# Attention scores as three fp32r terms on stacked rows, head outputs feature-major in column halves, and new state-space and gate stages in a hybrid decoder block

## The chip, the cores and the metric

The kernel runs on one core of one Trainium2 chip. A core has a matrix engine (TensorE, here PE; its weight loads are listed apart as PEld), a vector engine (VectorE, DVE), an activation engine (ScalarE, ACT), GpSimd (POOL) and SyncE (SP), which here only issues transfers. Each engine works its instructions off in the order in which the program holds them. The metric is device microseconds of one execution; lower is better.

## The reference

One decoder layer on 512 tokens of width 2048, everything in float32:

```
h = rms_norm(x);  q, k, v, u = split(h @ W_in)
attention, 16 heads of 64:  q, k rms-normed per head
    logits = q.k * scale - slope_h * distance, causal;  softmax;  @ v
state space, 64 groups of 16 channels, 64 complex states per group:
    scan over tokens;  y = Re(C s) + D u;  g = gelu(y)
    s_out = g * sigmoid(g @ W_glu + b)
x = x + concat(rms_norm(attn), rms_norm(s_out)) @ W_out
x = x + relu(rms_norm(x) @ W1)^2 @ W2          (W1: 2048 x 8192)
```

With 512 tokens in two blocks of 256 the block selection of the reference keeps every past block, so attention is plain causal attention with a linear distance penalty.

## The kernel before, in words

All matrix products with a weight matrix are made of three fp32r matmuls. A float32 operand is split into a rounded high part and the remainder, both in fp32r, and low times high, high times low and high times high are summed (`panel`, L114). `load_w` brings 256 rows of 512 weight columns with one transfer on SP's queue, `split_w` (L105) makes the two parts (copy on ACT, subtraction on DVE), and each step of 128 rows issues 12 matmuls of 512 columns into four PSUM banks.

The order of work on each engine is written by a planner when the program is built: it replays the program in a timing simulation of its own and gives each free engine the ready instruction that stands first in the program; what lies in `with hi()` goes first. So the program order is attention first and the next panel second, and on PE the panel's matmuls fill in wherever attention's next step is not ready.

The stages, in program order:

1. **State space** (`build`, `run`, `post`, L441 to L562), 16 rounds of four groups, among the two u panels (`uproj`) and the panels of the first half of q, k, v. `build` makes per-round matrices: four float32 matmuls into `kps` (L482), one after the other in 16 partitions of the bank, one copy to `kev`, a transfer to memory and back as `m3`. `run` brings in the tokens, makes `vps` (L513, two groups in the lower and upper 64 partitions), runs the scan on DVE and makes `yps` (L542 and L543, 64 output partitions, one group after another), which one copy brings to `ysb`. `post` transposes and applies GELU with three ACT and three DVE operations (L556 to L562); it stores twice the GELU, and later steps multiply by 0.5.
2. **Head norms** (`head_norm_T`, L623): for each of four row blocks of q and k, sum of squares per head, a reciprocal square root by integer guess and three Newton steps (`rsqrt_mean`, L168, 14 small DVE instructions), scaling, transposes.
3. **Attention** (L671), two halves of four head pairs. For each pair, each of four row blocks `i` and each head `e`: scores in float32 on the 64 rows of that head (L685), `sps`; one DVE operation that adds the penalty and takes the row minimum (L690; q is negated, so scores have the other sign); exponential on ACT with row sums (L692); transposes of the tile (`pps`, L696); a copy (L698); outputs in float32 with the transposed probabilities as weights and 64 columns of v moving (L701). At the end of a pair the outputs are divided by the row sums and stored token-major in `o_sb`. POOL makes the two heads' penalty tiles (L679). `sps`, `pps` and `ops` have one PSUM bank each, the score tile `sm` three buffers. The first half stands ahead of the panels of the second half of q, k, v; the second half stands ahead of the gate's panels (L733) and the panels of W_out for the state-space part (L772).
4. **Gate** (L732): one over one plus exp(-x) by ACT, an addition and a DVE reciprocal, times the GELU, split into high and low.
5. **W_out**: four panels on the state-space rows ("z"), then the attention outputs are transposed (L795), scaled and split, and four panels follow on the attention rows ("a").
6. **Feed-forward**, L830 to the end.

Thirteen buffers of 1 MB (`page`) hold the large activations; a tile that asks for one waits until one is free. `x1`, four pages loaded from memory on SP's queue, is needed where the z panels are added to the residual.

Of the kernel before, what the change touches and what calls it, by code (L numbers as in the profile page):

```python
# [45 lines left out]
def hybrid_block_kernel(ctx, tc, x, norm1_gain, w_in, q_norm_gain, k_norm_gain,  # L46
# [121 lines left out]
    def rsqrt_mean(dst, ssq, n, shape):  # L168

        v = small.tile(shape, F32, name="rv", tag="rv")  # L170
        w = small.tile(shape, F32, name="rw", tag="rw")
# [55 lines left out]
    nbglu = const.tile([P, 8], F32, name="nbglu")  # L227
# [9 lines left out]
    with ExitStack() as sx:  # L237
# [203 lines left out]
        def build(b):  # L441
# [37 lines left out]
            S.copy(bst[LO, :, 1], bbi[HI, js])  # L479
            kps = aux("kps", "bx")  # L480
            for q in range(4):
                PE.matmul(kps[:GH, q * P:(q + 1) * P], bst[:, q // 2, q % 2, :],  # L482
                          s2[:, q // 2, q % 2, 0:8, :].rearrange("p s h -> p (s h)"), start=True, stop=True)
            kev = st("kev", (GH, 8, 4, GH))
            S.copy(kev, kps[:GH].rearrange("p (g s h) -> p s g h", g=4, s=8))
# [17 lines left out]
        def run(b, ysb):  # L503
# [34 lines left out]
            V.tensor_add(xs[LO, :, 1, 1:], a1[HI, 1], a2[HI, 1])  # L538
            yps = aux("yp", "rx")
            for q in range(4):  # L540
                o = yps[:NCH, q * P:(q + 1) * P]
                PE.matmul(o, u[:, q, :], m3[:, :, q, :], start=True, stop=False)  # L542
                PE.matmul(o, xs[:, q // 2, q % 2, 0:NCH],  # L543
                          s2[:, q // 2, q % 2, 1:9, :], start=False, stop=True)
            hf = b % 2
            S.copy(ysb[:, :, 4 * hf:4 * hf + 4, :],
                   yps[:NCH].rearrange("c (g t h) -> c t g h", g=4, t=TC))

        def post(k, ysb):
# [5 lines left out]
            y = st("sy", (P, 512), bufs=2)  # L555
            S.copy(y, ps)  # L556
            a = st("sy", (P, 512), bufs=2)
            S.activation(a, y, AF.Square)
            V.tensor_scalar(a, a, 0.044715, 1.0, op0=ALU.mult, op1=ALU.add)
            V.tensor_mul(a, a, y)  # L560
            S.activation(a, a, AF.Tanh, scale=math.sqrt(2.0 / math.pi))
            V.scalar_tensor_tensor(s0t(k), a, 1.0, y, op0=ALU.add, op1=ALU.mult)  # L562
# [45 lines left out]
        V.tensor_scalar(nbglu, vt[:, 32:40], -1.0, None, op0=ALU.mult)  # L608
# [14 lines left out]
    def head_norm_T(ps4, dst, gain):  # L623
        for m in range(4):
# [5 lines left out]
            ss = small.tile([P, 8], F32, name="ss", tag="ss")  # L630
            V.tensor_reduce(ss, sq.rearrange("p (h d) -> p h d", d=DH), axis=AX.X, op=ALU.add)
            rs = small.tile([P, 8], F32, name="rs", tag="rs")
            rsqrt_mean(rs, ss, DH, [P, 8])
            qv = q.rearrange("p (h d) -> p h d", d=DH)
            V.tensor_mul(qv, qv, bc(rs, 2, DH))
            ps = ax("qt")
            for pr in range(4):
                PE.transpose(ps[:, pr * P:(pr + 1) * P], q[:, pr * P:(pr + 1) * P], ident)
# [30 lines left out]
    o_sb = [ap_.tile([P, 2, 1024], F32, name=f"o{i}") for i in range(2)]  # L669

    def attention(hf, qT, kT, vv):  # L671
        for pr in range(4):
            ops = aux("ops", "ops")
            rsum = small.tile([P, 4, 2], F32, name="rsum", tag="rsum")
            pen = []
            for e in range(2):
                slope = 2.0 ** (-8.0 * (hf * 8 + 2 * pr + e + 1) / H)
                pen.append(ap_.tile([P, 512], F32, name="pen", tag="pen", bufs=2))
                G.tensor_scalar(pen[e], dist, slope, 0.0, op0=ALU.mult, op1=ALU.add)  # L679
            for i in range(4):  # L680
                n = (i + 1) * P
                for e in range(2):
# [376 lines left out]
```

## Time and profile before

| | |
|---|---|
| median of 3 runs | 2156.73 us (2155.82 to 2157.74) |
| profiled execution | 2154.98 us |
| its span, first to last instruction | 2153.1 us |
| PE busy | 2113.7 us (98%) |
| DVE busy | 1517.7 us (70%) |
| ACT busy | 818.6 us (38%) |
| POOL busy | 199.6 us (9%) |
| granted PE clock, mean | 0.996 |

Busy time counts instructions from start to end; on PE they overlap, so the share says little on how close PE is to its rate, and the distance from one start to the next says more. A group's row gives line, engine, operation, tiles, shapes, count, then busy time and mean nanoseconds of one, then the idle time of the engine just before and what ended it. A float32 matmul is listed as two instructions, an fp32r matmul as one.

### The profile page before, as it was taken

The numbers are of one execution on the slowest core, as the hardware profiler recorded it, in microseconds if no ns is written. First come the engines' busy times: TensorE is split into PE (matmuls) and PEld (weight loads), VectorE is DVE, ScalarE is ACT, GpSimd is POOL, SyncE is SP. The second block draws the span as 40 slices with busy tenths as digits, with TensorE's granted clock in tenths as the row PEclk, the third lists the DMA queues.
The fourth block names the chain that finished last, engine by engine and source line by source line (L and its number), as shares of the span: only waits on it lengthen the run. The fifth ranks groups of instructions, "written<-read, shape, count | busy, mean of one in ns | idle before, by whom it ended". The sixth has DMA issues, their size and how long they took to land.

```text
span 2153.1 us, 26096 instructions
## 1 busy us (share of the span) xinstructions
PE 2113.7 (98%) x9905; PEld 1711.1 (79%) x9905; DVE 1517.7 (70%) x2514; ACT 818.6 (38%) x1295; POOL 199.6 (9%) x291
## 2 busy tenths in 40 slices
PE   8889999999999999999999999999999999999998
PEld 6667777777777888888888888888888888888887
DVE  6889993435475444677777777777777777877767
ACT  5233443444454343333333333333333333333332
POOL 1486650000020000000000000000000000000000
PEclk9999999999999999999999999999999999999999
DMA  6332222212132441233332333333333333333332
GB/s 196 108 91 86 80 89 88 69 59 69 59 118 78 135 140 40 82 104 96 110 104 92 117 98 98 118 98 98 115 101 98 108 108 98 99 114 97 95 114 98
DMA packets 149613, 213.51 MB, mean 99 GB/s; under 512 B 15672, under 2 KB 82320, under 8 KB 148976
## 3 DMA queue, kind: packets, MB, share of 16 engines
q1 hardware_dynamic: 136240, 201.36, 29.7%
q10 hardware_dynamic: 12416, 8.92, 1.4%
q0 software_dynamic: 832, 1.57, 0.3%
q8 instruction: 78, 1.28, 0.3%
q14 instruction: 47, 0.39, 0.1%
HBM read 204.54 MB, written 7.27 MB: 98 GB/s over the span
## 4 chain that ended last, share of the span: by engine, by line
PE 87%; DVE 8%; issue 1%; DMA 1%; POOL 1%; ACT 1%; SPq 0%; ACTq 0%; DVEq 0%; POOLq 0%
PE f L865 11%; PE f L866 11%; PE f L867 11%; PE g L961 9%; PE g L963 9%; PE g L959 9%; PE mm L133 6%; PE mm L132 6%; PE mm L134 6%; PE sps L685 2%; PE ops L701 2%; PE mm L136 1%; DVE wl L111 1%; PE mm L137 1%; PE mm L138 1%
## 5 line engine op out<-in xcount | busy, mean ns | idle before, releaser
L846 ACT CAST th<-w 128x1024 fp32r<-128x1024 f32 x349 | 361.7, 1054 | 644.9 <-PE g L963 467.3
L847 DVE TENSOR_TENSOR tl<-w,th 128x1024 fp32r<-128x1024 f32 x349 | 425.9, 1221 | 63.0 <-ACT th L846 63.0
L969 DVE TENSOR_TENSOR x<-x,g 128x512 f32<-128x512 f32 x434 | 294.0, 684 | 241.3 <-PE g L963 240.7
L865 PE MATMUL f<-h2h,tl 128*128 128x512 f32 x1024 | 398.5, 389 | 0.0
L866 PE MATMUL f<-h2l,th 128*128 128x512 f32 x1024 | 398.5, 389 | 0.0
L867 PE MATMUL f<-h2h,th 128*128 128x512 f32 x1024 | 398.4, 389 | 0.0
L961 PE MATMUL g<-tl,lf 128*128 128x512 f32 x868 | 337.9, 389 | 0.5 <-DVE tl L847 0.5
L963 PE MATMUL g<-th,lf 128*128 128x512 f32 x868 | 337.7, 389 | 0.0
L959 PE MATMUL g<-th,lf 128*128 128x512 f32 x868 | 320.0, 389 | 0.0
L111 DVE TENSOR_TENSOR wl<-raw,wh 128x512 fp32r<-128x512 f32 x208 | 150.9, 730 | 170.5 <-ACT wh L110 170.0
L867 PEld LDWEIGHTS f<-h2h,th 128*128 128x128 f32 x1024 | 192.2, 188 | 39.9
L865 PEld LDWEIGHTS f<-h2h,tl 128*128 128x128 f32 x1024 | 192.2, 188 | 39.8
L866 PEld LDWEIGHTS f<-h2l,th 128*128 128x128 f32 x1024 | 192.2, 188 | 39.8
L110 ACT CAST wh<-raw 128x512 fp32r<-128x512 f32 x208 | 128.3, 620 | 201.9 <-PE mm L134 127.5
L961 PEld LDWEIGHTS g<-tl,lf 128*128 128x128 f32 x868 | 162.9, 188 | 35.0 <-DVE tl L847 1.3
L959 PEld LDWEIGHTS g<-th,lf 128*128 128x128 f32 x868 | 163.0, 188 | 33.8
L963 PEld LDWEIGHTS g<-th,lf 128*128 128x128 f32 x868 | 162.9, 188 | 33.8
L132 PE MATMUL mm<-wh,xl 128*128 128x512 f32 x384 | 153.9, 402 | 0.5 <-DVE sy L582 0.5
L133 PE MATMUL mm<-wl,xh 128*128 128x512 f32 x384 | 154.2, 402 | 0.0
L134 PE MATMUL mm<-wh,xh 128*128 128x512 f32 x384 | 153.7, 401 | 0.0
L874 ACT ACTIVATE r<-r 128x512 f32<-128x512 f32 x64 | 40.0, 628 | 146.5 <-DVE r L873 146.5
L133 PEld LDWEIGHTS mm<-wl,xh 128*128 128x128 f32 x384 | 72.5, 189 | 21.5 <-issue 7.5
(344 smaller groups left out, 2723.4 us busy)
## 6 DMA issues: line engine op xcount, KB each, us to landing
w<-in_w_ff_dram SPq DMA_DIRECT2D x256, 512.0 KB, 3.8
raw<-in_w_in_dram SPq DMA_DIRECT2D x64, 512.0 KB, 3.7
raw<-in_w_out_dram SPq DMA_DIRECT2D x32, 512.0 KB, 3.6
x<-in_x_dram SPq DMA_DIRECT2D x7, 1024.0 KB, 11.7
m<-kp ACTq DMA_DIRECT2D x16, 256.0 KB, 3.3
raw<-in_w_glu_dram SPq DMA_DIRECT2D x8, 512.0 KB, 3.6
out_dram<-x SPq DMA_DIRECT2D x16, 256.0 KB, 2.2
ud<-sy ACTq DMA_DIRECT2D x8, 256.0 KB, 2.1
```

The source lines that it names most:

```text
L132: PE.matmul(ps[m], xl[:, ms], wh, start=st, stop=False)
L133: PE.matmul(ps[m], xh[:, ms], wl, start=False, stop=False)
L134: PE.matmul(ps[m], xh[:, ms], wh, start=False, stop=sp)
L846: S.copy(th, src)
L847: V.tensor_sub(tl, src, th.bitcast(F32))
L865: PE.matmul(ps[m], wl[:, k % 4, ms], xh_, start=k == 0, stop=False)
L866: PE.matmul(ps[m], wh[:, k % 4, ms], xl_, start=False, stop=False)
L867: PE.matmul(ps[m], wh[:, k % 4, ms], xh_, start=False, stop=k == 15)
L959: PE.matmul(ps[t], al_, th[:, q, :], start=first and q == 0, stop=False, skip_group_check=True)
L961: PE.matmul(ps[t], ah_, tl[:, q, :], start=False, stop=False, skip_group_check=True)
L963: PE.matmul(ps[t], ah_, th[:, q, :], start=False, stop=q == 1, skip_group_check=True)
L969: V.tensor_add(xs, xs, ps[t])
```

## The change

- **Scores.** `head_parts` makes, for each head, a tile `qhl` of 128 rows: the high part of q (divided by the head's slope) in its own 64 rows, the low part in the other 64; `khh`, the high part of k in both; `klo`, the low part of k in its own rows and zeros in the others. Two fp32r matmuls over 128 rows then give high.high + low.high + high.low. The DVE operation multiplies the penalty by the slope itself, so POOL's penalty tiles go.
- **Normalisation ahead.** The reciprocal of the row sum is taken per tile on DVE, and POOL scales the probabilities before they are transposed.
- **Outputs feature-major.** v is now the weight (64 columns) and the transposed probabilities move (128 columns); the two heads of a pair write the lower and upper 64 partitions of one bank, issued in turn. A copy on ACT stores the pair in `oraw`; the transposes ahead of the a panels go. The squares for the row norm are summed over features and brought into a row sum by small matmuls with ones (`row_rstd`), as for the state-space part.
- **State space.** `kps` writes four groups of 32 partitions, with four copies instead of one; `yps` writes two halves of 64 partitions, with two copies. GELU is one activation (tanh form) from PSUM into its place, without the factor two.
- **Head norms.** One `rsqrt_mean` for the four row blocks of a panel instead of four.
- **Gate.** The four banks of a panel are copied by DVE into a page, then four sigmoids follow on ACT; squares for the norm go from ACT to DVE. The split of the GELU's output goes wholly to DVE.

```diff
@@ build
-                PE.matmul(kps[:GH, q * P:(q + 1) * P], bst[:, q // 2, q % 2, :],
+                PE.matmul(kps[32 * q:32 * q + GH, 0:P], bst[:, q // 2, q % 2, :],
...
-            S.copy(kev, kps[:GH].rearrange("p (g s h) -> p s g h", g=4, s=8))
+            for q in range(4):
+                S.copy(kev[:, :, q, :], kps[32 * q:32 * q + GH, 0:P].rearrange("p (s h) -> p s h", s=8))
@@ run
-            for q in range(4):
-                o = yps[:NCH, q * P:(q + 1) * P]
-                PE.matmul(o, u[:, q, :], m3[:, :, q, :], start=True, stop=False)
-                PE.matmul(o, xs[:, q // 2, q % 2, 0:NCH],
-                          s2[:, q // 2, q % 2, 1:9, :], start=False, stop=True)
+            for j in range(2):
+                o = [yps[64 * e:64 * e + 64, j * P:(j + 1) * P] for e in range(2)]
+                for e in range(2):
+                    PE.matmul(o[e], u[:, 2 * j + e, :], m3[:, :, 2 * j + e, :], start=True, stop=False)
+                for e in range(2):
+                    PE.matmul(o[e], xs[:, j, e, 0:NCH], s2[:, j, e, 1:9, :], start=False, stop=True)
...
@@ post
-            y = st("sy", (P, 512), bufs=2)
-            S.copy(y, ps)
-            a = st("sy", (P, 512), bufs=2)
-            S.activation(a, y, AF.Square)
-            V.tensor_scalar(a, a, 0.044715, 1.0, op0=ALU.mult, op1=ALU.add)
-            V.tensor_mul(a, a, y)
-            S.activation(a, a, AF.Tanh, scale=math.sqrt(2.0 / math.pi))
-            V.scalar_tensor_tensor(s0t(k), a, 1.0, y, op0=ALU.add, op1=ALU.mult)
+            S.activation(s0t(k), ps, AF.Gelu_apprx_tanh)
@@ attention
+    def head_parts(qT, kT, pr, e, inv):
+        own, oth = slice(e * DH, (e + 1) * DH), slice((1 - e) * DH, (2 - e) * DH)
+        qhl = ap_.tile([P, 512], F32R, name="qhl", tag="qhl", bufs=2)
+        khh = ap_.tile([P, 512], F32R, name="khh", tag="khh", bufs=2)
+        q, k = qT[own, pr, :], kT[own, pr, :]
+        S.activation(qhl[own], q, AF.Copy, scale=inv)
+        V.scalar_tensor_tensor(qhl[oth], q, inv, qhl[own].bitcast(F32), op0=ALU.mult, op1=ALU.subtract)
+        V.tensor_copy(khh[own], k)
+        V.tensor_copy(khh[oth], k)
+        V.tensor_sub(klo[e][own], k, khh[own].bitcast(F32))
+        return qhl, khh
...
-                    PE.matmul(sps[:, :n], qT[rows, pr, i * P:(i + 1) * P], kT[rows, pr, 0:n],
-                              start=True, stop=True)
+                    PE.matmul(sps[:, :n], qhl[:, i * P:(i + 1) * P], khh[:, 0:n], start=True, stop=False)
+                    PE.matmul(sps[:, :n], qhl[:, i * P:(i + 1) * P], klo[e][:, 0:n], start=False, stop=True)
...
+                    rinv = small.tile([P, 1], F32, name="rinv", tag="rinv")
+                    V.reciprocal(rinv, rsum)
+                    G.tensor_scalar(sm[:, :n], sm[:, :n], rinv, 0.0, op0=ALU.mult, op1=ALU.add)
...
-                    for b in range(i + 1):
-                        PE.matmul(ops[:, o:o + DH], pt[:, b * P:(b + 1) * P],
+                for b in range(i + 1):
+                    for e in range(2):
+                        PE.matmul(oT[e * DH:(e + 1) * DH, i * P:(i + 1) * P],
                                   vv[:, b, pr * P + e * DH:pr * P + (e + 1) * DH],
-                                  start=b == 0, stop=b == i)
+                                  pts[e][:, b * P:(b + 1) * P], start=b == 0, stop=b == i)
+            with hi():
+                S.copy(oraw[:, pr, :], oT)
@@ gate
+        gate = page("gate")
+        with hi():
+            for m in range(4):
+                V.tensor_copy(gate[:, m, :], ps[m])
+            for m in range(4):
+                S.activation(gate[:, m, :], gate[:, m, :], AF.Sigmoid, bias=vt[:, 32 + 4 * n + m:33 + 4 * n + m])
...
-                e = t2("ge")
-                S.activation(e, ps[m], AF.Exp, bias=nbglu[:, k:k + 1], scale=-1.0)
-                V.tensor_scalar(e, e, 1.0, None, op0=ALU.add)
-                V.reciprocal(e, e)
@@ ahead of the a panels
-    for k in range(8):
-        ps = aux("ot", "tx")
-        for i in range(4):
-            PE.transpose(ps[:, i * P:(i + 1) * P], o_sb[i // 2][:, i % 2, k * P:(k + 1) * P], ident)
-        scaled_split(ah[k // 4][:, k % 4, :], al[k // 4][:, k % 4, :], ps, ga[:, k:k + 1])
+    for k in range(8):
+        o = oraw[k // 4][:, k % 4, :]
+        scaled_split(ah[k // 4][:, k % 4, :], al[k // 4][:, k % 4, :], o, ga[:, k:k + 1])
+        if k == 0:
+            S.activation(rbc, o, AF.Square)
+        else:
+            oq = t2("oq")
+            S.activation(oq, o, AF.Square)
+            G.tensor_add(rbc, rbc, oq)
+    rstda = row_rstd(rbc, "a")
```

More of the change, by code (lines that the diff above doesn't have):

```diff
@@ L168, in rsqrt_mean @@
     def rsqrt_mean(dst, ssq, n, shape):
-        v = small.tile(shape, F32, name="rv", tag="rv")
-        w = small.tile(shape, F32, name="rw", tag="rw")
+        v = ssq
+        w = small.tile([P, 32], F32, name="rw", tag="rw", bufs=1)
+        w = w[:, :math.prod(shape[1:])]
+        if len(shape) == 3:
+            w = w.rearrange("p (a b) -> p a b", b=shape[2])
         V.tensor_scalar(v, ssq, 1.0 / n, EPS, op0=ALU.mult, op1=ALU.add)
@@ L226, in hybrid_block_kernel @@
     kgain = vt[:, 41:42]
-    nbglu = const.tile([P, 8], F32, name="nbglu")
     qgain = const.tile([P, 1], F32, name="qgain")
@@ L623, in head_norm_T @@
     def head_norm_T(ps4, dst, gain):
+        qs = []
+        ss = small.tile([P, 4, 8], F32, name="ss", tag="ss", bufs=1)
         for m in range(4):
@@ L668, in hybrid_block_kernel @@
                     fill=1e33, base=384, channel_multiplier=1)
-    o_sb = [ap_.tile([P, 2, 1024], F32, name=f"o{i}") for i in range(2)]
-    def attention(hf, qT, kT, vv):
-        for pr in range(4):
[L673 to L679, printed above, removed]
+    klo = [ap_.tile([P, 512], F32R, name=f"klo{e}") for e in range(2)]
@@ new lines, in hybrid_block_kernel @@
+    for e in range(2):
+        V.memset(klo[e].bitcast(F32)[(1 - e) * DH:(2 - e) * DH], 0.0)
+    def head_parts(qT, kT, pr, e, inv):
[9 more added lines that the diff above has]
+        return qhl, khh
@@ L680, in attention @@
+    def attention(hf, qT, kT, vv, oraw):
+        for pr in range(4):
+            oT = aux("ops", "ops")
+            slope = [2.0 ** (-8.0 * (hf * 8 + 2 * pr + e + 1) / H) for e in range(2)]
+            parts = [head_parts(qT, kT, pr, e, 1.0 / slope[e]) for e in range(2)]
             for i in range(4):
                 n = (i + 1) * P
+                pts = []
                 for e in range(2):
-                    rows = slice(e * DH, (e + 1) * DH)
+                    qhl, khh = parts[e]
@@ L691, in attention @@
                                            op0=ALU.add, op1=ALU.min, accum_out=mn)
-                    S.activation(sm[:, :n], sm[:, :n], AF.Exp, bias=mn, scale=-1.0,
-                                 accum_out=rsum[:, i, e:e + 1])
+                    rsum = small.tile([P, 1], F32, name="rsum", tag="rsum")
+                    S.activation(sm[:, :n], sm[:, :n], AF.Exp, bias=mn, scale=-1.0, accum_out=rsum)
+                    rinv = small.tile([P, 1], F32, name="rinv", tag="rinv")
+                    V.reciprocal(rinv, rsum)
@@ L720, in hybrid_block_kernel @@
         with hi():
-            S.activation(h_, s0t(k), AF.Copy, scale=0.5)
-            V.scalar_tensor_tensor(l_, s0t(k), 0.5, h_.bitcast(F32), op0=ALU.mult, op1=ALU.subtract)
-    attention(1, *qkv1)
+            V.tensor_copy(h_, s0t(k))
+            V.tensor_sub(l_, s0t(k), h_.bitcast(F32))
+    oraw.append(page("oraw1"))
+    attention(1, *qkv1, oraw[1])
     def sact(k):
@@ L733, in hybrid_block_kernel @@
         ps = panel(w_glu, 0, 8, n * 512, sact, False)
+        gate = page("gate")
+        with hi():
+            for m in range(4):
+                V.tensor_copy(gate[:, m, :], ps[m])
+            for m in range(4):
+                S.activation(gate[:, m, :], gate[:, m, :], AF.Sigmoid, bias=vt[:, 32 + 4 * n + m:33 + 4 * n + m])
         for m in range(4):
```

82 lines of the change are left out of this document (35 added, 47 removed).

## The prediction

> **What bounds the kernel now.** I read the page first (busy shares, the forty slices, the chain), then a table of stretches, then the order of time on the matrix engine (PE).
>
> ```profile
> PE 2113.7 (98%) x9905; PEld 1711.1 (79%) x9905; DVE 1517.7 (70%) x2514; ACT 818.6 (38%) x1295; POOL 199.6 (9%) x291
> PE   8889999999999999999999999999999999999998
> DVE  6889993435475444677777777777777777877767
> PE 87%; DVE 8%; issue 1%; DMA 1%; POOL 1%; ACT 1%; SPq 0%; ACTq 0%; DVEq 0%; POOLq 0%
> ```
>
> PE is the chain for 87% of the span. The other 13% lies almost all in the first six slices, where DVE has 8s and 9s. The stretches below (columns: length, then busy time of PE, PEld, DVE, ACT, POOL, each with its count) are: the state-space stage with the u and first q, k, v projections; the attention stage; the remainder of the z projection; the feed-forward network.
>
> ```profile
> 85.00:323.00 238.00, 222.69 (x1359) 171.35 (x1358) 214.49 (x547) 95.97 (x211) 155.85 (x236) 0.98 0.30 88
> 358.00:688.00 330.00, 327.93 (x1579) 247.99 (x1579) 164.29 (x415) 148.65 (x334) 20.91 (x21) 1.00 0.24 75
> 688.00:741.00 53.00, 53.00 (x250) 44.17 (x250) 25.76 (x52) 18.91 (x38) 0.00 (x0) 1.00 0.28 90
> 813.00:2153.10 1340.10, 1333.75 (x5899) 1103.37 (x5897) 1000.38 (x1190) 472.35 (x547) 0.00 (x0) 1.00 0.32 100
> ```
>
> In 85 to 323 us PE (223 of 238) and DVE (214 of 238) are both nearly full: relieving one alone gives little there. In 358 to 741 PE has no idle time to speak of, and DVE and ACT are half idle: a microsecond of PE work less is a microsecond less, as long as other matmuls cover attention's waits. The last 1340 us hold nothing that the diff touches.
>
> How much cover is there? The two rows below are the projection matmuls alone, in the attention stage and in the stretch after it.
>
> ```profile
> 358.00:688.00 330.00, 234.94 (x934) 169.40 (x933) 2.72 (x4) 14.58 (x22) 1.00 0.24 75
> 688.00:741.00 53.00, 50.52 (x219) 40.89 (x219) 7.12 (x11) 0.00 (x0) 1.00 0.28 90
> ```
>
> For 64 score tiles (16 heads, 4 row blocks) 934 were used, 14.6 per tile; 219 were left when attention ended. So there are 1153/64 = 18 per tile.
>
> **Prices on PE.** A busy PE overlaps its own tails, so I price by start to start.
>
> ```profile
> 396.38 0.39 PE L133 MATMUL mm<-wl,xh 128*128 128x512 f32 x1
> 396.60 0.39 PE L134 MATMUL mm<-wh,xh 128*128 128x512 f32 x1
> 396.92 1.12 PE L685 MATMUL sps<-kT,qT 64*128 64x512 f32 x2
> 397.98 0.50 PE L132 MATMUL mm<-wh,xl 128*128 128x512 f32 x1
> ...
> 407.53 1.00 PE L701 MATMUL ops<-vv,pt 128*128 128x64 f32 x8
> 408.37 0.61 PE L696 MATMUL pps<-ident,sm 128*128 128x128 f32 x4
> 408.90 0.48 PE L685 MATMUL sps<-kT,qT 64*128 64x128 f32 x2
> 409.32 0.50 PE L133 MATMUL mm<-wl,xh 128*128 128x512 f32 x1
> ...
> 292.96 0.38 PE L542 MATMUL yp<-m,u 128*64 128x128 f32 x2
> 294.27 0.38 PE L542 MATMUL yp<-m,u 128*64 128x128 f32 x2
> 294.58 0.50 PE L133 MATMUL mm<-wl,xh 128*128 128x512 f32 x1
> ...
> 303.39 0.73 PE L513 MATMUL vp<-u,m1t 128*64 128x64 f32 x16
> 304.05 0.50 PE L132 MATMUL mm<-wh,xl 128*128 128x512 f32 x1
> ```
>
> - An fp32r matmul of 512 columns steps 0.22 to 0.23 us: I use 0.227.
> - An fp32 pass of 128 columns (a float32 matmul is two instructions) steps 0.109: twelve between 292.96 and 294.27.
> - The change from 64 output columns to 128 costs: 294.27 plus two passes is 294.49, the next begins at 294.58, so 0.09 at each side of such a group. The same 0.09 lies between 396.60 + 0.227 and 396.92.
> - A score tile takes from 396.83 to 397.98 = 1.15 us at 512 keys. At 128 keys: four transposes from 408.37 end at 408.81, the next projection starts at 409.32, 0.51. On the line between them 256 and 384 keys are 0.72 and 0.94.
> - With weights of 128 columns a pass over only 64 costs (408.37 - 407.53)/8 = 0.105: that is the floor of one step.
> - vp writes its two heads' groups into column halves. Sixteen passes of 64 columns take 304.05 - 0.09 - 303.39 = 0.57 us; single file at half of 0.109 they would take 0.87. So halves overlap, by 1.53 here.
>
> The counts:
>
> ```profile
> L685 PE MATMUL sps<-kT,qT 64*128 64x128 f32 (+3 forms) x128 | 51.4, 482 | 1.1 <-DVE mn L690 1.0
> L701 PE MATMUL ops<-vv,pt 128*128 128x64 f32 x320 | 43.8, 268 | 0.6 <-ACT pt L698 0.6
> L543 PE MATMUL yp<-s,xst 128*64 128x128 f32 x128 | 26.9, 294 | 10.6 <-DVE xst L535 10.6
> L482 PE MATMUL kps<-s,bst 128*16 128x128 f32 x128 | 18.1, 281 | 2.2 <-DVE s L473 1.3 <-DVE s L474 0.8
> L795 PE MATMUL ot<-ident,o 128*128 128x128 f32 x32 | 4.0, 272 | 0.0
> ```
>
> **The change, part by part.**
>
> *Scores.* Now 16 x (0.51 + 0.72 + 0.94 + 1.15) = 53.1 us. After: two fp32r matmuls over all 128 rows, so no change of shape beside the projections. At 512 columns 0.227 each; in proportion 0.170 and 0.114, and the floor of 0.109 at 128: sum 0.62, twice, sixteen times, 19.8 us. Gain 33. No row shows fp32r under 512 columns; if it ran there at the float32 pace (two passes of 0.109 per 128 columns) the tiles would cost 48 and the gain be 5. The nearest row is the fp32r one: I take 33, bounds 5 and 34.
>
> *Outputs.* Now 320 x 0.105 = 33.6. After: 320 passes of 128 columns, two heads in column halves, and 32 groups with 2 x 0.09 at their sides. No overlap: 34.9 + 5.8 = 40.7, a loss of 7. Full overlap without a side cost: 17.4, a gain of 16. I take an overlap of 1.75, between vp's 1.53 and 2: 19.9 + 5.8 = 25.7, gain 8. The 32 transposes of L795 go (3.5), eight small passes for the row sums come (0.9): gain 2.6. **Attention on PE: 43 less**, 0.67 per tile.
>
> *State space on PE.* yp (L542 has as many as L543): 256 x 0.109 = 27.9; at 1.75, 12 less (bounds 0 and 14). kps in four column groups: 14 us; at an overlap of 2, 7 less (0 and 10.5). Sum 19.
>
> *State space on DVE.*
>
> ```profile
> L560 DVE TENSOR_TENSOR sy<-sy 128x512 f32<-128x512 f32 x8 | 5.4, 675 | 0.0
> L559 DVE TENSOR_SCALAR sy<-sy 128x512 f32<-128x512 f32 x8 | 4.2, 519 | 2.5 <-ACT sy L558 2.5
> L562 DVE SCALAR_TENSOR_TENSOR s0b<-sy 128x512 f32<-128x512 f32 x4 | 3.1, 784 | 0.0
> L179 DVE TENSOR_TENSOR rs<-rs,rw 128x8 f32<-128x8 f32 x24 | 4.1, 194 | 0.1
> L178 DVE TENSOR_SCALAR rw<-rw 128x8 f32<-128x8 f32 x24 | 3.0, 157 | 0.0
> ...
> L740 DVE RECIPROCAL ge<-ge 128x512 f32<-128x512 f32 x8 | 26.8, 3351 | 0.2
> ```
>
> The GELU leaves DVE: 5.4 + 4.2 + 8 x 0.76 = 15.7. The head norms call the 14-step reciprocal root twice instead of eight times here: 14 x 157 to 194 ns = 2.2 to 2.7 each, six fewer, 13. DVE 29 less, PE 19 less, each of 238. With today's idle time kept the PE bound is 19 shorter and the DVE bound 29: PE sets it. ACT gets four small copies for one in kev and two in ysb and loses two activations and a copy per GELU; it is busy 96 of 238, and that idle time hides it; on the path it would be about 0.5 us per build, 8 in all. I take **17 less** for the stage (bounds 3 and 24).
>
> *New links in attention's chain.* Between exponential and transpose stand a reciprocal (DVE) and a scaling of the tile (POOL). Ahead of each head stand one ACT and four DVE operations, and klo, qhl, khh have one buffer per head of the pair: they wait for the last score tile of the pair before, and the next pair's first scores queue behind them.
>
> ```profile
> L705 DVE RECIPROCAL rinv<-rsum x8: 138/203/205, 400.4 to 677.8; 128x8 f32<-128x8 f32 x8
> L679 POOL TENSOR_SCALAR pen<-dist x16: 620/622/1291, 342.2 to 640.9; 128x512 f32<-128x512 f32 x16
> 588.00:602.00 14.00, 3.06 (x13) 2.22 (x13) 0.00 (x0) 1.37 (x2) 1.00 0.01 1
> L685 PE MATMUL sps<-kT,qT x12: 272/481/693, 588.2 to 601.4; 64*128 64x256 f32 x4, 64*128 64x384 f32 x4, 64*128 64x128 f32 x2, 64*128 64x512 f32 x2
> L569 ACT ACT_TABLE_LOAD x1 | 1.3, 1283 | 7.2 <-DMA x<-in_x_dram 7.2
> x<-in_x_dram SPq DMA_DIRECT2D x7, 1024.0 KB, 11.7
> ```
>
> (The third row is the projections alone in 588 to 602 us, the fourth the scores there: six tiles.) That is 0.2 + 0.6 per tile and some 3 us per head, 0.76 per tile (0.63 on ACT as for one 512-wide activation; on DVE one as L562, one as L560, two as L559, 2.5): 1.5 us, or 6 projection matmuls. If the interval between tiles stays, the 0.67 us that PE saves takes 3 more matmuls per tile, 17.6, within the 18. If all 1.5 us show, it is 23.7 per tile: the cover ends after 1153/23.7 = 49 tiles, and 15 go bare. Today those six tiles went nearly bare beside some 13 projections: (14 - 3)/6 = 1.8 us a tile. Their PE work falls from 1.4 to 0.7, so 1.1 idle each: 17 us. Three buffers for the tile let much of it overlap: I take **8** (bounds 0 and 25).
>
> The Trainium skill, GPSIMD Engine Reference, section Key points, says that POOL shares its SBUF interfaces with VectorE and contends with two-input instructions there, which speaks against scaling on POOL. The row's longest, 1291 beside a median of 622, agrees; at that price all the time 0.6 us more per tile make 26 matmuls per tile, 20 bare tiles rather than 15, and the sum some 6 us worse.
>
> *Gate.* Four sigmoids per half need another table than the exponentials that run beside them: 2 to 8 loads per half at 1.28 us. ACT is idle 181 of the 330 us and hides them; bare, 4 loads cost 5 us. DVE loses the 3.35 us reciprocals (26.8) and the 13 of the second half's head norms; it gains the head parts (16 x 2.5 = 40), 64 small reciprocals (13), eight copies and eight squares (10): some 23 more on 164 of 330, covered.
>
> The Trainium skill, ScalarE: Activation LUTs, section What ACT_TABLE_LOAD costs, gives about 2.66 us for a switch with its drain. The trace has 1.28 and one load; by the page 16 loads would be 43 us of ACT, still inside the idle 181.
>
> *Pages.* oraw1 and the two gate pages are 3 more claims on 13 pages; x1 loads wait for sh and sl, and weight loads behind them on SP's queue wait too. The first z panel (20 us or more) covers it; bare, one 1 MB load would be 11.7 us.
>
> **Sum.** -43 - 17 + 8 = -52. The profiled execution is 2154.98 us (span 2153.1 and 1.9 around it), 1.75 under the median of 2156.73. So 2103 for the profiled one, 2104.7 against the median: **2105**.
>
> **The rivals.**
> 1. *All of PE's saving is kept*: cover holds, and the stage gives 19 to 24: 2156.7 - 43 - 22 = 2092 or a little lower, 2075 if the halves overlap fully as well (8 + 5 more, no side cost). For it: PE at 327.93 of 330, 219 matmuls over. Against: longer chain, less PE work per tile.
> 2. *The column halves do not overlap* with passes of 128 columns, the change then not doing what it says: outputs lose 7 instead of gaining 8, the stage gives 5: 2156.7 - 33 - 2.6 + 7 - 5 + 8 = 2131. Against it: vp's 16 in 0.57 us.
> 3. *Cover runs out early*: 25 rather than 8: 2121.
> 4. *Slower: attention becomes a serial chain.* If the planner puts a head's tiles one after another at the end, with nothing beside them, a tile costs its own latency: at 512 keys scores 0.5, reduction 0.8, exponential 0.9, reciprocal 0.2, scaling 0.6, transposes 0.6, copy 0.6, outputs 0.5, near 4.7, of which PE works 0.7: 4 us idle each. From 60/4 = 15 such tiles on the saving is gone; 25 would give 2156.7 - 60 + 100 = 2197. Against it: in 588 to 602 tiles overlapped, 1.8 us each.
>
> **How the numbers follow.** Forecast 0.49, rival 1 0.19, rival 2 0.08, rival 3 0.13, rival 4 0.08; 0.03 that gains and losses cancel. The kernel's runs lie within 0.1%; I count under 0.2% (4 us) as no change. Faster 0.89, same 0.03, slower 0.08. The range from 2074 (rival 1 at its end) to 2138 (scores at a smaller gain beside rival 2) leaves out rival 4 and the far bounds. The forecast's own range is 2090 to 2118.
>
> **What would show it.** Scores: 64 pairs of fp32r steps, 0.45 us at 512 keys and 0.22 at 128. Outputs: four passes in about 0.25 us. The last score tile at 620 to 650 us or, if cover fails, later, with PE digits under 9 after 600. The first score tile near 340 rather than 358. The feed-forward stretch stays 1340 us long. I am wrong if PE's idle time between 340 and 690 exceeds 30 us, if fp32r steps at 128 keys are above 0.2, or if the state-space stage keeps its 238 us.

## The result and the profile after

The changed kernel takes 2121.52 us (median of 4 runs, 2120.13 to 2121.9) where the kernel before took 2156.28 beside it (2154.06 to 2157.74): a ratio of 0.984, with an interval from 0.982 to 0.986. That is 35 us less; 52 less were forecast, 2105 in a range from 2074 to 2138.

From the page after: busy times, PE's forty slices, and the chain.

```profile
PE 2074.2 (98%) x9881; PEld 1680.6 (79%) x9881; DVE 1529.2 (72%) x2435; ACT 834.6 (39%) x1351; POOL 239.1 (11%) x346
PE   8899999999989999999999999999999999999998
PE 85%; DVE 10%; issue 1%; POOL 1%; DMA 1%; ACT 1%; SPq 0%; ACTq 0%; DVEq 0%; POOLq 0%
```

PE is still the chain. New is the 8 in the twelfth slice, about 583 to 636 us, inside attention. The same stretches as before, and the feed-forward network (columns: length, busy time and count of PE, PEld, DVE, ACT, POOL, then the granted clock):

```profile
85.00:323.00 238.00, 224.70 (x1429) 169.26 (x1429) 207.59 (x457) 104.34 (x268) 152.59 (x236) 0.97 0.33 97
358.00:688.00 330.00, 320.24 (x1606) 248.91 (x1605) 197.62 (x446) 165.62 (x350) 62.25 (x74) 0.97 0.24 80
688.00:741.00 53.00, 53.00 (x263) 43.27 (x262) 26.26 (x49) 21.50 (x37) 1.34 (x1) 1.00 0.55 179
801.20:2119.70 1318.50, 1312.17 (x5797) 1085.52 (x5795) 993.10 (x1179) 466.15 (x533) 0.00 (x0) 1.00 0.33 102
```

In the attention stretch PE is idle for 9.8 us (2.1 before), and the granted clock is 0.97 where it was 1.00. The first score tiles, before and after (order of time on PE, start first):

```profile
358.08 0.48 PE L685 MATMUL sps<-kT,qT 64*128 64x128 f32 x2
```
```profile
338.22 0.22 PE L701 MATMUL sps<-khh,qhl 128*128 128x128 f32 x1
338.28 0.45 PE L132 MATMUL mm<-wh,xl 128*128 128x512 f32 x1
```

960 projection matmuls stand ahead of it in either kernel, so the state-space stage gave 20 us. From there to the first matmul of the attention rows' W_out panels it was 383.6 us (358.1 to 741.6) and is 370.1 (338.2 to 708.4): 13.5 less. From that point to the end nothing has changed; the first feed-forward matmul comes at 801.2 instead of 834.6, 33.4 earlier, as does the end.

I split the 383.6 and 370.1 us by what PE had started, each instruction until the start of the next, without the idle time:

```
us on PE            before   after   forecast for the difference
projections          274.2   272.6     0
scores                47.3    26.5   -33
outputs               34.0    35.6    -8
tile transposes       18.8    21.0     0
ot, row sums           4.0     1.7    -2.6
idle                   2.1     9.8    +8 (exposed chain)
```

(The rest, 3 us, are the transposes of the second half's head norms.) By these rows the scores gave 21 of 33, the outputs nothing, and the idle time came as forecast, though from other places. A row holds its steps at half clock too, which the section on the prediction takes out.

How much cover attention used: projection matmuls (and the head of the W_out panels) between the first score tile and the last output, of the kernel after.

```profile
338.00:701.60 363.60, 278.00 (x1129) 209.53 (x1127) 13.76 (x20) 9.03 (x14) 0.97 0.25 82
701.60:708.40 6.80, 5.99 (x26) 4.67 (x26) 1.50 (x2) 0.00 (x0) 1.00 0.80 260
```

1129 over 64 tiles are 17.6 per tile, and 26 are left ahead of the panels on the attention rows: 17.6 of 18 were forecast (by luck, as shown below).

### The profile page after: what moved, and what is told of

Read it like the earlier page. It is cut to its first block, busy times and chain, and to the rows that moved or that the text cites. A ratio compares the mean times of both kernels' runs of the same rounds, so it can differ in the third digit from the quotient of the medians.

```text
span 2119.7 us, 26204 instructions
## 1 busy us (share of the span) xinstructions
PE 2074.2 (98%) x9881; PEld 1680.6 (79%) x9881; DVE 1529.2 (72%) x2435; ACT 834.6 (39%) x1351; POOL 239.1 (11%) x346
## 3 DMA queue, kind: packets, MB, share of 16 engines
q8 instruction: 78, 1.28, 0.3%
## 4 chain that ended last, share of the span: by engine, by line
PE 85%; DVE 10%; issue 1%; POOL 1%; DMA 1%; ACT 1%; SPq 0%; ACTq 0%; DVEq 0%; POOLq 0%
PE f L887 11%; PE f L888 11%; PE f L889 11%; PE g L983 9%; PE g L985 9%; PE g L981 9%; PE mm L132 5%; PE mm L133 5%; PE mm L134 5%; DVE wl L111 2%; PE ops L722 1%; PE mm L136 1%; PE mm L137 1%; PE mm L138 1%; PE pps L715 1%
## 5 line engine op out<-in xcount | busy, mean ns | idle before, releaser
L111 DVE TENSOR_TENSOR wl<-raw,wh 128x512 fp32r<-128x512 f32 x208 | 156.5, 756 | 119.2 <-ACT wh L110 118.2
L132 PEld LDWEIGHTS mm<-wh,xl 128*128 128x128 f32 x384 | 73.1, 190 | 17.6 <-issue 2.0
## 6 DMA issues: line engine op xcount, KB each, us to landing
x<-in_x_dram SPq DMA_DIRECT2D x7, 1024.0 KB, 11.5
```

The costliest lines, as they stand in the source:

```text
L132: PE.matmul(ps[m], xl[:, ms], wh, start=st, stop=False)
```

## Experiments

Every kernel was timed beside the kernel before. Where the text says "more" or "less" than another kernel, it is the difference of the two ratios, in us of 2156; the intervals are some 3 us to either side.

```
                                             median us   ratio [interval]
the change                                     2121.5    0.984 [0.982, 0.986]
scores undone                                  2141.3    0.993 [0.992, 0.995]
groups in single file                          2125.3    0.986 [0.985, 0.987]
old GELU and head norms                        2134.6    0.991 [0.989, 0.992]
old gate                                       2148.2    0.997 [0.996, 0.998]
whole output groups                            2107.6    0.978 [0.976, 0.979]
page early                                     2119.3    0.983 [0.982, 0.985]
squares later                                  2118.6    0.983 [0.981, 0.985]
whole groups + page early                      2109.5    0.979 [0.977, 0.980]
whole groups + squares later                   2103.3    0.976 [0.975, 0.977]
  and scaling on DVE                           2106.7    0.977 [0.975, 0.979]
  and scaling on DVE, page early               2106.6    0.977 [0.976, 0.979]
  and page early                               2105.6    0.977 [0.975, 0.979]
```

### Parts undone

**Scores.** The changed kernel with float32 scores on 64 rows:

```diff
-PE.matmul(sps[:, :n], qhl[:, ...], khh[:, 0:n], start=True, stop=False)
-PE.matmul(sps[:, :n], qhl[:, ...], klo[e][:, 0:n], start=False, stop=True)
+PE.matmul(sps[:, :n], qT[rows, pr, ...], kT[rows, pr, 0:n], start=True, stop=True)
```

> Scores as before the change: one float32 matmul on 64 rows per score tile, the penalty tiles made by POOL, no head parts; all else is as after. Theory (the scores' saving on the matmul engine reaches the end, at its measured size): the score steps rise from 26.5 to 47 us in sum, the time by 16 to 22 us to 2138 to 2143. Rival (the saving was lost in the bare tiles, whose chain is as long with either form, and the head parts cost DVE time in them): the time rises by 0 to 8 us, to at most 2130, and the idle time of the matmul engine falls by some 5 us.

2141.3, 20 us more, and the score steps are 47.1 us in sum: the size that the theory forecast. From the first score tile to the panels on the attention rows, after and then with the scores undone:

```profile
338.22:708.37 370.15, 360.39 (x1810) 281.17 (x1808) 213.40 (x477) 183.34 (x383) 64.82 (x78) 0.97 0.26 85
```
```profile
340.20:728.68 388.48, 387.14 (x1801) 273.25 (x1801) 181.04 (x417) 173.09 (x365) 69.51 (x92) 1.00 0.24 78
```

PE's idle time fell from 9.8 to 1.3 us and the clock stays at 1.00, so the exposed places belong to the new form. That the time nevertheless rises by just the score steps' 20 us is an accident of two more sums: about 15 us of PE work come back beside the scores, and as much idle time and half clock goes (the section on the prediction has the account).

**Column groups of the state-space stage.**

```diff
-PE.matmul(kps[32 * q:32 * q + GH, 0:P], ...)
+PE.matmul(kps[:GH, q * P:(q + 1) * P], ...)
```

(and yps alike, one copy for each again)

> kps and yps are made as before the change: four groups one after the other in the same 16 or 64 partitions, one copy each; all else is as after. Theory (the matmul engine set the state-space stage): the 20 us by which the first score tile came earlier (358.1 to 338.2) come back nearly whole, first score tile at 353 to 358 us, time up by 15 to 20 us to 2136 to 2142. Rival (DVE set the stage; its 29 us less work was the gain): the first score tile stays at 338 to 343 us and the time rises by 0 to 5 us.

2125.3, 4 us more, with intervals that overlap; the first score tile at 343.8. The other kernels with the stage as after have it anywhere from 337.3 to 341.8, so 2 to 6.5 us are this edit's. The rival: PE did not set the stage. What the edit costs PE in work it gets back in waiting. PE's longest wait in 85 to 323 us, after and then in single file:

```profile
PE yp L550 <- DVE xst L539: 4.7, 4, 2.2
```
```profile
PE yp L547 <- DVE xst L538: 2.8, 2, 2.5
```

All PE waits listed there add up to 12.8 us after and 5.7 in single file.

**GELU and head norms.**

```diff
-S.activation(s0t(k), ps, AF.Gelu_apprx_tanh)
+S.activation(y, ps, AF.Copy, scale=0.5)
+S.activation(a, y, AF.Square)
+V.tensor_scalar(a, a, ...); V.tensor_mul(a, a, y)
+S.activation(a, a, AF.Tanh, ...)
+V.scalar_tensor_tensor(s0t(k), a, 1.0, y, ...)
```

(and one `rsqrt_mean` for each row block)

> GELU by three activations and three DVE operations, and the head norms' reciprocal root once for each row block, as before the change (the factor one half goes into the first copy); all else is as after. The single-file groups cost the first score tile 5.6 us and the kernel 3.8. Theory (DVE set the state-space stage): the rest of the 20 us comes back, first score tile at 349 to 355 us, time up by 10 to 15 us to 2131 to 2137. Rival (the matmul engine set it, or both parts are needed together for any gain): first score tile at 338 to 345 us, time up by 0 to 6 us.

2134.6, 15 us more, the first score tile at 351.6, 13.4 later:

```profile
351.61 0.22 PE L705 MATMUL sps<-khh,qhl 128*128 128x128 f32 x1
```

PE's waits in 85 to 323 us add up to 24 us here (12.8 after): 10.5 for DVE, 6.0 for POOL, 5.5 for a transfer, 1.9 for ACT. So what the edit brings back, most of it work on DVE, held the stage up, in part through waits on other engines, which I have not followed further. The run does not separate the GELU from the head norms, nor DVE's operations from the two more activations that ACT has per GELU. The two edits add up to 19 us, about what the stage gave.

**Gate.**

```diff
-V.tensor_copy(gate[:, m, :], ps[m])
-S.activation(gate[:, m, :], gate[:, m, :], AF.Sigmoid, ...)
+S.activation(e, ps[m], AF.Exp, ...)
+V.tensor_scalar(e, e, 1.0, None, op0=ALU.add)
+V.reciprocal(e, e)
```

> The gate as before the change: exponential from the projections' banks, one added and the reciprocal taken on DVE, no gate page and no sigmoid; all else is as after. Theory of the prediction (the gate's change is covered on every engine and worth nothing): within 4 us of 2121.5. Rival (DVE is the bound of the gate's stretch, 28 to 29 of 30 us busy there, and 26.8 us of reciprocals would come back in it while the banks wait): more bare score tiles, the matmul engine idle by 10 us more, and the time up by 8 to 20 us to 2130 to 2141.

2148.2: 28 us more, beyond the rival's range. In this kernel the reciprocals, two windows of 30 us, and PE's two longest waits; then the same windows after:

```profile
L762 DVE RECIPROCAL ge<-ge x8: 3331/3352/3355, 540.8 to 639.9; 128x512 f32<-128x512 f32 x8
```
```profile
610.00:640.00 30.00, 21.55 (x112) 14.14 (x111) 28.89 (x55) 19.41 (x44) 10.12 (x12) 0.94 0.39 153
640.00:670.00 30.00, 20.89 (x108) 16.15 (x107) 27.65 (x37) 16.17 (x27) 13.03 (x10) 0.86 0.46 141
```
```profile
PE pps L717 <- POOL sm L714: 9.2, 9, 2.6
PE mm L132 <- DVE x L803: 9.1, 1, 9.1
```
```profile
610.00:640.00 30.00, 24.20 (x104) 18.22 (x103) 22.96 (x52) 13.82 (x31) 10.66 (x11) 0.83 0.12 42
640.00:670.00 30.00, 30.00 (x158) 23.67 (x157) 12.65 (x31) 12.05 (x28) 4.75 (x7) 1.00 0.28 89
```

With the old gate DVE is busy for 28.89 and 27.65 of 30 us. PE waits once 9.1 us for a bank that DVE sets free, and nine times for a tile that POOL scales after DVE's small reciprocal; from the first score tile to the feed-forward network it idles 27.7 us (9.8 after), and about 12.6 are lost at half clock (8.2 after). 684 projection matmuls are left when attention ends (409 after): cover was there, and was not issued. A full DVE alone does not stop PE, though: after, DVE is busy for 29.20 of the 30 us from 580 to 610 and PE for 29.98. Whether the longer time at this load does it, or single reciprocals of 3.35 us that hold up short steps behind them, is not shown. The four parts undone add up to 68 us, the change gave 35: no part has a price of its own. That they draw on the same DVE time and the same cover is my reading of it.

### Where the forecast gain went

**Whole output groups.** Order of time on PE, after (projections left out):

```profile
433.30 0.43 PE L722 MATMUL ops<-pt,vv 128*64 128x128 f32 x2
433.67 0.33 PE L701 MATMUL sps<-khh,qhl 128*128 128x128 f32 x1
...
438.63 1.09 PE L722 MATMUL ops<-pt,vv 128*64 128x128 f32 x14
439.65 0.33 PE L715 MATMUL pps<-ident,sm 128*128 128x128 f32 x1
```

Fourteen passes take 439.65 - 438.63 = 1.02 us, 0.073 each, where 0.109 is one pass alone: the halves overlap. But the first head's first pair of passes is issued alone, 5 us ahead of the rest, and takes 0.37 us: there are 64 groups, not 32. The edit issues the second head first:

```diff
 for b in range(i + 1):
-    for e in range(2):
+    for e in (1, 0):
         PE.matmul(oT[e * DH:(e + 1) * DH, ...], ...)
```

> The two heads' output matmuls are issued second head first, so that each of the 32 groups is issued whole instead of as one lone pass pair and a rest. Theory (the groups' edges ate the outputs' gain): 32 lone groups of about 0.4 us each shrink to two passes inside a group, the steps of the output matmuls fall from 35.6 us in sum to 23 to 26, the time by 9 to 12 us, from 2121.5 to 2110 to 2113. Rival (the column halves simply do not give more, the sum is set by the passes): the sum stays at 33 us or above and the time within 3 us of 2121.5. Second rival (attention's chain sets the end, and the first head's product now waits for the second head's tile): the matmul engine's idle time between first score tile and the attention panels, 9.8 us, grows by as much as the outputs gain, and the time stays or rises by up to 5 us.

2107.6, 13 us less than after. The output steps fall from 35.6 to 23.9 us in sum, in 32 groups. One group in order of time, and all of them as a group of instructions (busy time, mean, idle time before):

```profile
434.70 1.09 PE L722 MATMUL ops<-pt,vv 128*64 128x128 f32 x16
```
```profile
L722 PE MATMUL ops<-pt,vv 128*64 128x128 f32 x320 | 25.9, 294 | 2.7 <-ACT pt L717 2.7
```

Scores (26.5 to 24.2, 1.3 of it half clock) and tile transposes (21.0 to 16.9) fall too: 18 of the 64 tiles had their first score matmul right behind an output group, and now 2 have. Idle time grew only from 9.8 to 13.4: the second rival is out.

**The page.** From 537.6 to 556.1 us nine score tiles run with no projection beside them. DVE, after:

```profile
553.98 0.16 DVE L711 RECIPROCAL rinv<-rsum 128x1 f32<-128x1 f32 x1 [0.67 <-ACT sm L709]
554.06 2.46 DVE L757 COPY gate<-mm 128x512 f32<-128x512 f32 x4
```

The banks of the first gate panel were full when its last matmul started at 537.34, and their copies stand 17 us later in DVE's order. The pages of the gate stage are asked for after `oraw1`, and `oraw1` is first written at 556.1. (On the chip the first of these copies starts 2 us ahead of that write: what holds them back is their place in the planner's order, not a wait.)

```diff
 oraw.append(page("oraw1"))
+with hi():
+    V.memset(oraw[1][:, 0, 0:2], 0.0)
```

> Two elements of the page oraw1 are written by DVE with high priority at the place where the page is asked for, ahead of the second half of attention; nothing else is changed. Theory (the bare score tiles at 538 to 556 us stand there because the pages of the gate stage, which free the four PSUM banks of the projections, are handed out in program order behind oraw1, and that page is first written at 556 us): the projections run on through 538 to 556, the idle 3.9 us there and some 5 us lost at half clock go, and the time falls by 6 to 9 us to 2112.5 to 2115.5. Rival (cover is a fixed stock: what is used there is missing later, so that bare tiles only move to the end of attention): a time within 3 us of 2121.5, with as much idle time on the matmul engine. Third possibility: the stretch stays bare although the page is there, the banks being held for another reason; the time is unchanged.

The stretch is gone: PE is busy for all of 520 to 580 us at clock 1.00 (26.79 of 30 in 520 to 550 after). The cause of the stretch is thereby settled. The time is 2119.3, though, 1 to 2 us less, which the intervals can't tell from after. The rival holds: at the last output 300 matmuls are left instead of 409, and the end pays. From the last output to the feed-forward network (712.1 to 797.5) it takes 17.3 us beyond 0.227 for each of the 300; after (701.6 to 801.2) it was 6.8 beyond the 409. The same was seen with whole groups:

> Both the whole groups of output matmuls and the early write of the page. Theory (cover is a fixed stock; the page alone won 2 us because what it spent early was missing at the end): 2105 to 2110, no better than the whole groups alone at 2107.6. Rival (with less matmul work in attention the bare stretch at 520 to 550 us, 5.9 us idle and 3 us of half clock, goes without a new one): 2098 to 2102.

2109.5, no better than 2107.6. The end of attention in that kernel:

```profile
703.96 0.59 ACT L726 COPY oraw<-ops 128x512 f32<-128x512 f32 x1 [1.19 <-PE ops L722]
...
710.34 0.95 PE L781 MATMUL rps<-ones,rbc 128*128 128x2 f32 x8
...
714.83 2.73 DVE L842 SCALAR_TENSOR_TENSOR x<-mm,rstda,x 128x512 f32<-128x512 f32 x4
...
715.68 0.87 PE L834 MATMUL ht<-ident,x 128*128 128x128 f32 x3 [4.40 <-issue]
```

From the last outputs' copy to the first bank set free lie 12 us of one chain: split, squares, addition, row sums, fourteen steps, residual. In the kernel after, 26 spare matmuls and the first panel hide it; here nothing is left to.

**POOL beside DVE.** The largest hole of the kernel after, DVE, POOL and PE in order of time:

```profile
614.04 0.35 DVE L179 TENSOR_TENSOR rw<-rstds 128x8 f32<-128x8 f32 x1
614.34 5.33 POOL L817 TENSOR_TENSOR rbc<-rbc,oq 128x512 f32<-128x512 f32 x4
614.42 1.21 DVE L180 TENSOR_TENSOR rw<-rw,sss 128x8 f32<-128x8 f32 x1
615.66 0.17 DVE L181 TENSOR_SCALAR rw<-rw 128x8 f32<-128x8 f32 x1
615.87 1.11 DVE L182 TENSOR_TENSOR rstds<-rstds,rw 128x8 f32<-128x8 f32 x1
...
620.66 0.69 PE L701 MATMUL sps<-khh,qhl 128*128 128x384 f32 x1 [5.79 <-DVE mn L706]
```

While POOL adds, DVE's two-input steps on eight columns take up to 1.21 us; the one-input steps between them stay at 0.17. Each stretched step ends with one of POOL's four additions: they end at 615.60, 616.96, 618.32 and 619.66, the steps at 615.63, 616.98, 618.34 and 619.69. The tile's reduction stands behind this chain. The edit starts the additions after it:

```diff
+zb = const.tile([P, 1], F32, name="zb")
+V.tensor_scalar(zb, rstds[:, 0:1], 0.0, None, op0=ALU.mult)
-S.activation(rbc, o, AF.Square)
+S.activation(rbc, o, AF.Square, bias=zb)
```

> The first square of the attention rows takes its bias, a zero, from the finished reciprocal root of the gate rows (one tiny DVE operation more), so that POOL's additions of squares begin only after the 14-step chain of DVE and no longer beside it; the sums are the same. Theory (POOL's two-input additions stretch the two-input steps of that chain from 0.17 to 1.1 us, and the matmul engine waits 5.8 us behind them): the steps take 0.17 us, the hole of 5.8 us shrinks to 1.5 or less, the half clock of some 10 us after it goes with it, and the time falls by 6 to 10 us to 2111 to 2115. Rival (the chain's place ahead of the tile's reduction in DVE's queue makes the hole, POOL is a bystander): the hole keeps 4 us or more and the time falls by 0 to 2 us.

The same steps and the same wait in this kernel:

```profile
617.21 0.17 DVE L180 TENSOR_TENSOR rw<-rw,sss 128x8 f32<-128x8 f32 x1
617.41 0.17 DVE L181 TENSOR_SCALAR rw<-rw 128x8 f32<-128x8 f32 x1
617.62 0.17 DVE L182 TENSOR_TENSOR rstds<-rstds,rw 128x8 f32<-128x8 f32 x1
...
619.56 0.44 PE L701 MATMUL sps<-khh,qhl 128*128 128x384 f32 x1 [1.89 <-DVE mn L706]
```

Every step takes 0.17, the hole shrinks from 5.79 to 1.89, and the half clock after it from 10.2 to 3.4 us. The mechanism is shown; its worth, 2 us, is within the intervals, where 6 to 10 were expected. In the trace the stretch from first score tile to the panels is 5.6 us shorter (370.1 to 364.5), and 2.9 of that are lost ahead of the first score tile, which comes at 341.1 instead of 338.2, inside the scatter named above; why that scatters I have not found. On top of whole groups:

> Both the whole groups of output matmuls and the later additions of squares. Theory (POOL beside DVE's chain costs here too, 3.4 + 1.4 + 0.5 us idle at 605 to 612 us and 3 us of half clock after): the time falls by 4 to 8 us under the whole groups alone, to 2099.5 to 2103.5. Rival (the chain's place in the queue makes the holes): within 2 us of 2107.6.

2103.3: 4 us less than whole groups alone (the intervals overlap, but each of the four runs is under each of the other four), and the shortest time of all kernels here, 0.976 of before and some 17 us under the change. PE's idle time fell from 13.4 to 9.3.

**Scaling.** On that kernel, the added link moved:

```diff
-G.tensor_scalar(sm[:, :n], sm[:, :n], rinv, 0.0, op0=ALU.mult, op1=ALU.add)
+V.tensor_scalar(sm[:, :n], sm[:, :n], rinv, None, op0=ALU.mult)
```

> As the kernel with whole groups and later additions (2103.3 us), but the probabilities are scaled on DVE (a one-input operation with the reciprocal as scalar) instead of on POOL. Theory (the added link over POOL lengthens each tile's chain and takes cover): each tile needs fewer projection matmuls beside it, more than 412 of them are left when attention's last output is issued, the bare tiles idle less, and the time falls by 2 to 6 us to 2097 to 2101. Rival (DVE, with some 64 x 0.4 = 26 us more work in the attention stage, becomes the engine that others queue behind): the time rises by 0 to 6 us to as much as 2109.

2106.7, 2 us more and inconclusive by the intervals. 457 matmuls are left at the end instead of 412, so each tile does need less cover with the shorter chain; yet PE idles 11.5 us instead of 9.3, 4.2 of them waiting to transpose. Both halves of the expectations came true, and the rival's weighs as much.

> The same with the page written early. Theory (what the early page spends was missing at the end, where the row norm of the attention rows and its 14-step chain stood bare beside 300 matmuls after the last output; with a shorter chain per tile more than that is left): the bare stretch at 520 to 550 us goes, the end is covered, and the time is 4 to 9 us under the kernel without the early page, 2090 to 2097. Rival (cover is a fixed stock and the end pays what the middle gains, as in the two runs with the page before): within 3 us of the kernel without the early page.

2106.6: the same as without the page; at the last output 300 matmuls are left again.

> Whole groups, later additions of squares (POOL scales, as in the change) and the page written early. Theory (cover is a fixed stock; with 300 projection matmuls after the last output the row norm's chain stands bare there): 2101 to 2106, within 3 us of the same without the page, 2103.3. Rival (the page's gain comes through once the additions no longer collide): 2095 to 2099.

2105.6, with the page no better than 2103.3 without it, 300 matmuls left. Four kernels have the page early, and none gained more than its interval by it.

## Why the prediction was right or wrong

The time came out inside the range, 16.5 us over the forecast. Taken apart on PE, with idle time and half clock set aside (the clock is treated under Exposure), from the first score tile to the panels on the attention rows:

```
us                        before   after   scores undone   whole groups
the stretch                383.6   370.1       388.5          355.9
PE idle                      2.1     9.8         1.3           13.4
lost at half clock             0     8.2           0            5.7
PE's work at full clock    381.5   352.1       387.2          336.8
```

The sum was -43 - 17 + 8 = -52; measured it is about -29 (attention's work on PE), -20 (state space) and +16 (exposure) = -33.

**State-space stage: right in size (-17; 20 measured), wrong in its mechanism.** The step "PE bound 19 shorter, DVE bound 29 shorter: PE sets it" failed. It compared two busy sums, 223 and 214 of 238, as if either engine could run without the other. The engines wait for each other round after round; undoing PE's part cost 4 us, undoing DVE's (with its links through ACT) 15. PE busy for 224.70 of 238 after says the same: cover filled what was freed.

**Scores: right on PE; the table's -21 against -33 misleads.** Undoing them adds 35 us of work at full clock: 23 in the score steps (47.1 instead of 26.5, of which 2.0 are half clock), the rest in the steps beside them, 10 of it at the projections. The forecast of 33 had the size. Of it 17 were lost again as idle time and half clock. The old price of 53 includes an edge of 0.09 ahead of each tile; the table books it with what stands there, a projection or a transpose, which leaves 47.3. The step "no change of shape beside the projections" holds: between projections a pair costs 0.45 at 512 columns, as forecast. Behind an output group, where 18 of the 64 stand, it costs 0.57. One of each, in order of time after:

```profile
372.33 0.39 PE L133 MATMUL mm<-wl,xh 128*128 128x512 f32 x1
372.56 0.39 PE L701 MATMUL sps<-khh,qhl 128*128 128x512 f32 x1
372.78 0.39 PE L702 MATMUL sps<-klo,qhl 128*128 128x512 f32 x1
373.01 0.39 PE L134 MATMUL mm<-wh,xh 128*128 128x512 f32 x1
...
421.52 0.43 PE L722 MATMUL ops<-pt,vv 128*64 128x128 f32 x2
421.88 0.50 PE L701 MATMUL sps<-khh,qhl 128*128 128x512 f32 x1
422.21 0.40 PE L702 MATMUL sps<-klo,qhl 128*128 128x512 f32 x1
422.45 0.40 PE L134 MATMUL mm<-wh,xh 128*128 128x512 f32 x1
```

Two numbers of the working were off without weight. At 128 columns a step can be shorter than the "floor" of 0.109: the very first score matmul steps 0.06 (338.22 to 338.28). And the lower bound's cost of 48 is 49 with the 0.109 that it names.

**Outputs: the step "32 groups" failed.** Passes, overlap and side cost were sized well: 25.7 us were forecast and 23.9 measured once the groups are whole. (The overlap of 1.53 for vp was read against single-file passes of 64 columns at half of 0.109, which no row shows. Fourteen passes of 128 columns in 1.02 us, less two edges of 0.09, are 0.060 each: an overlap of about 1.8, beside the 1.75 assumed.) The planner issues whatever is ready, one head's tile is ready ahead of the other's, and so 64 groups were issued: 35.6 us, no gain. Mending this one step brought 13 us, most of the 17 by which the forecast was off. The work on PE then is 44.7 us under before, where 43 were forecast. Rival 2 (halves do not overlap) is excluded by 14 passes in 1.02 us.

**Exposure: 8 forecast, 16 measured.** 7.7 us are idle time and 8.2 half clock. That the idle time alone comes to 7.7 is luck, and so is the cover of 17.6 matmuls per tile: its premise, the interval between tiles staying while PE's work per tile falls by 0.67, failed on both sides. From the first score tile to the last output it took 330 us before (358.1 to 688.3) and takes 363 after (338.2 to 701.6), and attention's own steps fell by 0.27 per tile (1.56 to 1.30). The idle time stands in two places that I had not seen: the page order (I had named the page's claim, and hidden it beside "the first z panel") and POOL against DVE's small steps (I had weighed POOL against DVE for the scaling only, not for the sums of squares). What I left out altogether is the clock. The 3.4 us ahead of each fall and the 10.2 us of half clock behind it, first at the page's stretch, then at POOL's:

```profile
545.62:549.03 3.41, 1.74 (x17) 1.19 (x16) 3.25 (x8) 1.90 (x4) 1.12 (x1) 1.00 0.00 0
549.03:559.27 10.24, 9.50 (x39) 7.02 (x38) 4.99 (x18) 5.74 (x13) 1.93 (x4) 0.50 0.00 1
613.88:617.29 3.41, 0.99 (x6) 0.39 (x4) 3.21 (x7) 1.82 (x5) 3.24 (x4) 1.00 0.42 147
617.29:627.53 10.24, 6.87 (x20) 4.59 (x21) 9.56 (x23) 3.80 (x9) 4.67 (x5) 0.50 0.15 53
```

The busy time at half clock is 9.50 and 6.87 us; at full clock that work would take about half as long, so by this estimate 8.2 us are lost on top of the idle time. They sit in the rows of scores, outputs, transposes and projections of the first table. The Trainium skill, TensorE: Matmul & The Clock Gate, Part 1, has the clock halved after an idle window of about 3.4 us and back after as long a busy one. The return agrees: in the last 3.41 us of both stretches PE is busy throughout. The fall does not quite: PE was busy for 1.74 of the 3.41 us before the first, in gaps of at most 0.9 us, and for 0.99 before the second, which came 2.4 us into the hole.

**Gate: the step "covered, worth nothing" failed most.** Undone, it costs 28 us. I had DVE's sum over the whole stage (some 23 more on 164 of 330; it became 33), where the gate is a stretch of 100 us with attention beside it and, with the old gate, DVE at 28 of 30 us. Table loads beside attention were as few as forecast: 7 of 1.28 us.

**Rivals.** Nothing of the serial chain (4) was seen. Cover running out (3) had the right time, 2121, and only part of the mechanism: matmuls were left, but were not issued for want of banks. All of PE's saving kept (1) needed what the two edits above provide; whole groups alone came to 2107.6, beside the forecast of 2105.

**What would have shown me wrong:** PE's idle time stayed under 30 us and most steps at 128 keys under 0.2, as forecast; the last score tile came at 679 instead of 620 to 650.

## What to carry to other kernels

When two operations are to run side by side on PE, see in the order as issued that they stand side by side: a planner that takes what is ready splits the pair, and the program's order can forbid it. Filler work is a stock: count what one unit uses and what is left at the end before moving work into a bare stretch, because the tail has a chain of its own to hide. And a sum of busy time over a stage hides a stretch in which a second engine is full; size a change to that engine on windows no longer than the stretch. Before a difference is put down to one kind of step, take idle time and half clock out: here a change worth 35 us on PE showed as 21 in its own row and as 20 in the time.

## What the runs showed of the hardware

- Passes of 128 columns in two column halves: fourteen took 1.02 us, 1.5 times as fast as one after the other (1.53) with the group's edges in the time; four column groups brought the busy time of kps from 18.1 to 7.7 us.
- POOL's two-input additions on 128x512 stretched two-input DVE steps on 128x8 from 0.17 to as much as 1.21 us and left one-input steps at 0.17. The Trainium skill, GPSIMD Engine Reference, section Key points, has POOL and VectorE share SBUF interfaces, with contention for instructions with two inputs; the trace agrees, and an operation on eight columns pays nearly the time of one of POOL's.
- PE's clock fell to half after 3.41 us in which PE was busy for 1.74, in gaps none of which was longer than 0.9 us, and stayed there for 10.2 us.
